# Layer 0 of a two-layer trunk: other places for the scan turns, the first gate blocks and the first out-projection blocks

## The chip, the cores and the metric

The kernel runs on one core of one Trainium2 chip. The metric is the device time of one execution in microseconds (us); several executions give a median.

## The reference, cut to what matters

A trunk of two layers works on x of 1024 positions by 1024 channels in float32. Layer 0 is a state-space mixer (SSD), layer 1 a retention mixer; each is added to the residual stream, and a final norm follows. The change touches layer 0 and the start of its out-projection:

```
z, xbc, dt = split(rmsnorm(x) @ w_in)        # 2048 + 4096 + 32 columns
xs, B, C   = split(silu(causal_conv4(xbc)))  # 2048 + 1024 + 1024
y = ssd_scan(xs, softplus(dt + bias), B, C)  # chunks of 128, 8 groups of 4 heads
y = (y + d_skip * xs) * silu(z)
y = group_rmsnorm(y, 8 groups)
h = x + y @ w_out                            # contraction over 2048
```

Within a chunk the scan needs products of C and B weighted by a decay, and across chunks a state that is carried from one chunk to the next.

## The kernel before, in words

**Data and blocks.** Channels lie on partitions, positions on the free axis. Every product in float32 is made of three matmuls (mm3, L143): operand high by high, high by low, low by high, where high and low are an FP32R copy on ScalarE (L109) and the rest on VectorE (L110). A *block part* is one 128-column slice of w_in: B, C, two x slices and two z slices per group. Each block part is made in two *half blocks*, one for each half of the positions: 24 matmuls of 128x512 into one PSUM bank of the tag mm, which has three banks (project, L239). VectorE scales each bank by the norm's factor as it leaves PSUM (L342 for B, C and x; L363 for the gate z).

**Convolution.** After its second half block a B, C or x part goes through the causal convolution (conv_unit, L330): ScalarE starts an accumulator of the tag acc (L345), VectorE adds three taps (L347), ScalarE takes a tanh (L349), and VectorE finishes silu (L350). The tag acc has two buffers, and the norm's two squares use the same tag (L513).

**Turns of the scan.** Each of the 8 groups has 4 turns (visit, L441) of two chunks. A turn makes the state products pst (L461), then the PE part of the *next* turn's front (front_pe, L388: transposes of X and B and the product of B and C, L396 to L398), then the outputs py (L485, L491). The next turn's front on the other engines follows (front, L401): scaled copies of X (L414, L416), ScalarE's decay products (L425 to L433) and VectorE's products (L434, L436). The decays are loaded from DRAM by load_decay (L380, queue of SP) into the tag acb with two buffers, two turns at a time. The last turn of a group needs B, C and x of the following group, since it makes that group's first front.

**Norm of a group.** norm (L507) has three steps: the product with the gate (L511); squares on ScalarE and their sum on GpSimd (L515, L516); then matmuls pn with a matrix of ones (L522), a logarithm and an exponential on ScalarE (L523, L524), the scaling (L527) and the store to DRAM (L530, to ysp).

**The order.** Layer0.run (L533) merges generators: merge (L71) always advances the one with the smallest (steps done + 0.5) / length. In stage g (0 to 6) it merges the six block parts of the list steps[g + 1] (B, C, x, x of group g + 1 and z, z of group g; 12 half blocks, 10 in stage 0), the 4 turns of group g and the norm of group g - 1. In manual_schedule (L558) TensorE issues in this written order. All other engines and queues, and TensorE outside that part, are ordered by a planner that simulates the program; a buffer of a tag is waited for when all are in use.

**Start.** B and C of group 0 come first; then decay() (L259: the softplus of dt on VectorE and ScalarE, the running sums pcum and ptot on TensorE, both in mm banks, L303 to L306) is merged with x(0,0), x(0,1) and z(0,0) (L554). Then the front of the first turn is made (L559).

**Tail.** The last stage has the two z parts of group 7, its four turns, the norms of groups 6 and 7, and the first steps of the out-projection (OutProj, L575). One step of the out-projection is half of the contraction (8 of 16 slices) of one 128-row block of h for one half of the positions: 24 matmuls. A block's two halves follow one another in the same mm bank, and take_h (L675) adds the residual as the bank is read. The y values come back from ysp by DMA (load, L585: two slices each, y0 to y7) and are split into high and low. Loads y0 and y1 are issued ahead (start, L978), y2 to y6 as the contraction reaches them, and y7, which holds group 7, last (L610).

The merges of the stages, before:

```
lst = self.steps[g + 1]
gens = [(self.units(lst), 2 * len(lst)), (take(vs, 4), 4)]
if g:
    gens.insert(0, (self.norm(g - 1, 0, T), 4))
merge(*gens)
```

Of the kernel before, what the change touches and what calls it, by code (L numbers as in the profile page):

```python
# [20 lines left out]
P = 128  # L21
T = 1024
D = 1024
KT = D // P
NC = T // P
HALF = 512
# [42 lines left out]


def merge(*seqs):  # L71
    gens = [[iter(g), n, 0] for g, n in seqs]
    while gens:
        gens.sort(key=lambda e: (e[2] + 0.5) / e[1])
        e = gens[0]
        try:
            next(e[0])
            e[2] += 1
        except StopIteration:
            gens.pop(0)  # L80


def take(gen, n):
    for _ in range(n):
        if next(gen, StopIteration) is StopIteration:
            return
        yield


def urgent(tc, gen):  # L90
    while True:
        with tc.high_priority():
            if next(gen, StopIteration) is StopIteration:
                return
        yield
# [7 lines left out]
def drain(gen):  # L103
    for _ in gen:
        pass
# [7 lines left out]
class WStream:  # L113


    def __init__(self, nc, cx, srcs, ahead, name, pools=None):
        self.nc, self.cx, self.srcs, self.ahead, self.name = nc, cx, srcs, ahead, name
        self.pools = pools or [(cx.gp, 2)]
        self.ring = [pl for pl, n in self.pools for _ in range(n)]
        self.ready, self.next = [], 0  # L120
# [22 lines left out]
def mm3(nc, ps, ahi, alo, bhi, blo, first, last):  # L143
    nc.tensor.matmul(ps, ahi, bhi, start=first, stop=False)  # L144
    nc.tensor.matmul(ps, ahi, blo, start=False, stop=False)  # L145
    nc.tensor.matmul(ps, alo, bhi, start=False, stop=last)  # L146


class Layer0:
    def __init__(self, tc, cx):  # L150
        self.tc, self.cx, nc = tc, cx, tc.nc
        self.nc = nc
        con = cx.con
        self.es = ExitStack()
        self.ps = self.es.enter_context(tc.tile_pool(name="ps0", bufs=1, space=PSUM))
        self.sb = self.es.enter_context(tc.tile_pool(name="sb0", bufs=1, side="right"))
        self.ident = con[:, CO["ident"] : CO["ident"] + P]
        self.ones, self.ones_r = cx.ones, cx.ones_r
        self.tri = con[:, CO["tri"] : CO["tri"] + P]
        idx = {}  # L160
        for g in range(SSD_G):
            for j in range(2):
                idx[("z", g, j)] = 2 * g + j
                idx[("x", g, j)] = 16 + 2 * g + j
            idx[("B", g)] = 32 + g
            idx[("C", g)] = 40 + g
        self.steps = [[("B", 0), ("C", 0), ("x", 0, 0), ("x", 0, 1), ("z", 0, 0)]]
        for g in range(SSD_G):
            nxt = [("B", g + 1), ("C", g + 1), ("x", g + 1, 0), ("x", g + 1, 1)] if g + 1 < SSD_G else []
            self.steps.append(nxt + ([("z", g, 0), ("z", g, 1)] if g else [("z", 0, 1)]))  # L170
        seq = [s for st in self.steps for s in st]
        self.ws = WStream(nc, cx, [cx.w0[idx[s]] for s in seq], 1, "w0")
        self.S = [dict() for _ in range(SSD_G)]
        self.rstd = self.tile([P, T], "rstd", 1, "rstd0")
        self.dt_ps, self.first_banks = {}, []
# [357 lines left out]
    def run(self, tail, start):  # L533

        nc, cx = self.nc, self.cx
        self.load_x()
        self.split_x(0)
        self.dt_project(0)
        self.squares(0)
        first, second = self.units([("B", 0)]), self.units([("C", 0)])  # L540
        fb = self.ps.tile([P, 2, 512], F32, tag="pa", bufs=1, name="fb")
        self.first_banks = [fb[:, 0, :], fb[:, 1, :]]
        next(first)
        next(second)
        self.stats(0)
        self.split_x(1)
        self.dt_project(1)
        self.squares(1)
        next(first)
        next(second)  # L550
        self.stats(1)
        drain(first)
        drain(second)
        merge((self.decay(), 3), (self.units(self.steps[0][2:]), 2 * len(self.steps[0][2:])))  # L554
        for q in range(2):
            self.load_decay(0, q)
        vs = self.visits()
        with self.tc.manual_schedule(engines={mybir.EngineType.PE}):  # L558
            self.fr = self.front(0, 0, self.front_pe(0, 0))  # L559
            for g in range(SSD_G - 1):  # L560
                lst = self.steps[g + 1]
                gens = [(self.units(lst), 2 * len(lst)), (take(vs, 4), 4)]
                if g:
                    gens.insert(0, (self.norm(g - 1, 0, T), 4))
                merge(*gens)
            g = SSD_G - 1
            start()
            merge((self.norm(g - 1, 0, T), 4), (self.units(self.steps[g + 1]), 4), (take(vs, 2), 2))
        merge((take(vs, 1), 1), (self.norm(g, 0, HALF), 3), (take(tail, 1), 1))
        merge((vs, 1), (take(tail, 3), 3))  # L570
        merge((self.norm(g, HALF, T), 3), (tail, 4))
        self.es.close()


class OutProj:  # L575
    def __init__(self, tc, cx, wsrc, ysrc, name, slots, early, raw, evac):
        self.raw = raw
        self.tc, self.cx, self.nc = tc, cx, tc.nc
        self.ws = WStream(
            tc.nc, cx, [wsrc[d][i] for _ in range(2) for d in range(KT) for i in range(2)], 1, name  # L580
        )
        self.ysrc, self.name, self.slots, self.early, self.evac = ysrc, name, slots, early, evac
        self.ys = {}

# [13 lines left out]

    def gen(self):
        nc, cx = self.nc, self.cx  # L600
        for h in range(2):
            for d in range(KT):
                pt = cx.mm_tile(f"{self.name}p{h}_{d}")
                for i in range(2):
                    w = self.ws.get()
                    for kk in range(8):
                        k = 8 * i + kk
                        if kk % 2 == 0:
                            for a in range(k // 2, min(k // 2 + 2, 8)):
                                if h or a < 7 or k == 14:  # L610
                                    self.load(h, a)
                        hi, lo = self.ys[h, k // 2]
                        ks = slice(kk * P, (kk + 1) * P)
                        mm3(nc, pt, w[0][:, ks], w[1][:, ks], hi[:, k % 2, :], lo[:, k % 2, :], k == 0, k == 15)
                    if i == 1:
                        self.evac(h, d, pt)
                        a = d - (KT - 1 - len(self.early))
                        if h == 0 and 0 <= a < len(self.early):
                            self.load(1, a, self.early[a])
                    yield  # L620


class Rope:
# [43 lines left out]
class Layer1:  # L667
# [46 lines left out]
    def start(self):  # L714
        tc, cx = self.tc, self.cx
        self.es = ExitStack()
        self.ps = self.es.enter_context(tc.tile_pool(name="psL", bufs=1, space=PSUM))
        self.sb = self.es.enter_context(tc.tile_pool(name="sbL", bufs=1, reuse_waits="tile"))
        self.es.enter_context(tc.tile_pool(name="spad", bufs=1)).tile([P, 48], F32, name="spad")
        self.gB = self.es.enter_context(tc.tile_pool(name="gB", bufs=1, reuse_waits="tile"))  # L720
        seq = []
        for h in range(RH):
            seq += [cx.w1qk[4 * h + i] for i in range(4)]
            seq += [cx.w1g[4 * h + i] for i in range(4)]
            seq += [cx.w1v[4 * h + i] for i in range(4)]
        self.ws = WStream(self.nc, cx, seq, 1, "w1", [(cx.gp, 2), (self.gB, 3)])
# [211 lines left out]
def body(tc, aps):  # L938
    nc = tc.nc
    cx = Ctx()  # L940
# [3 lines left out]
    with ExitStack() as es:  # L944
# [27 lines left out]
        cx.act = act_es.enter_context(tc.tile_pool(name="actp", bufs=1))  # L972
        l0 = Layer0(tc, cx)
        l1 = Layer1(tc, cx)
        op0 = OutProj(tc, cx, aps["w0o"], cx.ysp, "o0", lambda i: (cx.act, "act", 16), [], lambda h: (l0.sb, "yT", 4), l1.take_h)
        g0 = op0.gen()

        def start():  # L978
# [108 lines left out]
```

## Time and profile before

| | us |
|---|---|
| Median of 3 runs | 1778.81 |
| Lowest and highest run | 1775.88, 1779.36 |
| The profiled execution's own time | 1781.39 |
| Its span in the trace | 1779.6 |
| TensorE busy in it | 1715.4 |
| VectorE busy | 1086.1 |
| ScalarE busy | 697.1 |

The span is what the trace covers, from the first to the last instruction; the execution's own time has a little around it. Engines are called PE (TensorE matmul), PEld (its weight load), DVE (VectorE), ACT (ScalarE), POOL (GpSimd) and SP (SyncE, which issues most DMAs). PEclk is the clock granted to TensorE as a share of 2.4 GHz. L12 is line 12 of the kernel. A wait is put down to what ended it last.

### The profile page before, as it was taken

Reading aid. Unit: us, or ns where it says so; the run is one execution under the profiler, and the core shown is the slowest. Engines: PE = TensorE matmul, PEld = TensorE weight load, DVE = VectorE, ACT = ScalarE, POOL = GpSimd, SP = SyncE. Lnnn points to the kernel's source line nnn. Section 1 sums busy time; section 2 is a strip of 40 time slices with the busy share of each in tenths; the row PEclk is TensorE's granted clock in tenths of the full one; section 3 lists DMA queues with packets and bytes.
Section 4 is the critical chain, followed back from the end, with each engine's and each line's share of the span. In section 5 each row is a group of like instructions: output and inputs, shape, how many; then the busy total and the mean of one; then the engine's idle time right before and its main releaser. Section 6 shows DMA issues by size and latency. Waiting matters only on the chain.

```text
span 1779.6 us, 21284 instructions
## 1 busy us (share of the span) xinstructions
PE 1715.4 (96%) x8382; PEld 1403.9 (79%) x8382; DVE 1086.1 (61%) x1681; ACT 697.1 (39%) x1066; POOL 100.8 (6%) x109
## 2 busy tenths in 40 slices
PE   8799999999999999899999999999999999999996
PEld 5677878787878787788878888888888888888885
DVE  7767677777777778667644157436624661666443
ACT  6344455454545455645431223132213322333422
POOL 3010101010101011100000000000000000000000
PEclk9899999999999999999999999999999999999998
DMA  5151222222222223456441102111211211344452
GB/s 181 34 104 63 60 83 61 83 71 72 72 80 63 83 61 95 143 185 217 142 151 51 48 13 77 54 48 33 75 36 54 66 51 45 112 134 140 152 177 78
DMA packets 74357, 157.69 MB, mean 89 GB/s; under 512 B 7568, under 2 KB 24592, under 8 KB 74256
## 3 DMA queue, kind: packets, MB, share of 16 engines
q1 hardware_dynamic: 72960, 154.09, 27.4%
q10 hardware_dynamic: 1296, 2.23, 0.3%
q8 instruction: 66, 1.08, 0.3%
q14 instruction: 35, 0.29, 0.1%
HBM read 130.99 MB, written 25.30 MB: 88 GB/s over the span
## 4 chain that ended last, share of the span: by engine, by line
PE 78%; DVE 11%; ACT 6%; DMA 3%; issue 1%; SPq 0%; DVEq 0%; ACTq 0%
PE ip L144 6%; PE ip L145 6%; PE ip L146 6%; PE o1p L146 3%; PE g L146 3%; PE g L145 3%; PE o1p L144 3%; PE g L144 3%; PE o1p L145 3%; PE v L144 3%; PE v L145 3%; PE v L146 3%; PE o0p L145 3%; PE o0p L146 3%; PE o0p L144 3%; DVE acc L347 2%
## 5 line engine op out<-in xcount | busy, mean ns | idle before, releaser
L144 PE MATMUL ip<-hh,w0h 128*128 128x512 f32 x496 | 196.8, 397 | 1.4 <-DVE pre L342 1.4
L145 PE MATMUL ip<-hl,w0h 128*128 128x512 f32 x496 | 194.6, 392 | 0.0
L146 PE MATMUL ip<-hh,w0l 128*128 128x512 f32 x496 | 193.9, 391 | 0.0
L110 DVE TENSOR_TENSOR w1l<-w1r,w1h 128x1024 fp32r<-128x1024 f32 x48 | 58.3, 1222 | 147.5 <-ACT w1h L109 146.9
L347 DVE SCALAR_TENSOR_TENSOR acc<-pre,vec,acc 128x1024 f32<-128x1024 f32 x96 | 122.5, 1278 | 6.6 <-ACT acc L345 5.9
L109 ACT CAST w0h<-w0r 128x1024 fp32r<-128x1024 f32 x48 | 50.4, 1049 | 188.4 <-PE ip L145 157.9
L144 PEld LDWEIGHTS ip<-hh,w0h 128*128 128x128 f32 x496 | 93.7, 189 | 24.6 <-issue 1.9
L145 PEld LDWEIGHTS ip<-hl,w0h 128*128 128x128 f32 x496 | 93.8, 189 | 20.2 <-DVE hl L215 0.8
L146 PEld LDWEIGHTS ip<-hh,w0l 128*128 128x128 f32 x496 | 93.7, 189 | 20.0 <-issue 0.2
L144 PE MATMUL o0p<-o0yh,o0h 128*128 128x512 f32 x256 | 101.5, 397 | 3.4 <-ACT o0yh L109 2.2
L342 DVE TENSOR_TENSOR pre<-ip,rstd 128x512 f32<-128x512 f32 x62 | 42.6, 688 | 101.2 <-PE ip L146 101.1
L109 ACT CAST w1h<-w1r 128x1024 fp32r<-128x1024 f32 x48 | 50.1, 1051 | 137.5 <-PE q L145 53.1
L146 PE MATMUL o0p<-o0yh,o0l 128*128 128x512 f32 x256 | 101.9, 398 | 0.6 <-DVE o0l L110 0.6
L144 PE MATMUL z<-hh,w0h 128*128 128x512 f32 x256 | 102.5, 400 | 0.0
L145 PE MATMUL o0p<-o0yl,o0h 128*128 128x512 f32 x256 | 101.1, 395 | 0.8 <-DVE o0yl L110 0.8
L144 PE MATMUL v<-w1h,h 128*128 128x512 f32 x256 | 101.6, 398 | 0.0
L146 PE MATMUL o1p<-o1yh,o1l 128*128 128x512 f32 x256 | 100.1, 392 | 0.4 <-DVE o1l L110 0.4
L145 PE MATMUL v<-w1l,h 128*128 128x512 f32 x256 | 100.3, 392 | 0.0
L146 PE MATMUL v<-w1h,h 128*128 128x512 f32 x256 | 100.1, 391 | 0.0
L144 PE MATMUL g<-w1h,h 128*128 128x512 f32 x256 | 100.0, 391 | 0.0
L146 PE MATMUL z<-hh,w0l 128*128 128x512 f32 x256 | 99.8, 390 | 0.0
L144 PE MATMUL o1p<-o1yh,o1h 128*128 128x512 f32 x256 | 99.6, 390 | 0.2 <-DVE vl L791 0.2
(242 smaller groups left out, 4000.3 us busy)
## 6 DMA issues: line engine op xcount, KB each, us to landing
w0r<-w SPq DMA_DIRECT2D x48, 512.0 KB, 3.3
acb<-acd SPq DMA_DIRECT2D x16, 1024.0 KB, 8.0
o0r<-w0o SPq DMA_DIRECT2D x32, 512.0 KB, 3.3
o1r<-w1o SPq DMA_DIRECT2D x32, 512.0 KB, 3.2
o0yr<-ysp SPq DMA_DIRECT2D x32, 256.0 KB, 3.4
w1r<-w1qk SPq DMA_DIRECT2D x16, 512.0 KB, 3.3
w1r<-w1g SPq DMA_DIRECT2D x16, 512.0 KB, 3.3
w1r<-w1v SPq DMA_DIRECT2D x16, 512.0 KB, 3.2
```

The costliest lines, as they stand in the source:

```text
L109: nc.scalar.copy(hi, src)
L110: nc.vector.tensor_tensor(lo, src, hi.bitcast(F32), ALU.subtract)
L144: nc.tensor.matmul(ps, ahi, bhi, start=first, stop=False)
L145: nc.tensor.matmul(ps, ahi, blo, start=False, stop=False)
L146: nc.tensor.matmul(ps, alo, bhi, start=False, stop=last)
L342: nc.vector.tensor_tensor(pre[:, 3 + h * HALF : 3 + (h + 1) * HALF], pt, self.rstd[:, sl], ALU.mult)
L347: nc.vector.scalar_tensor_tensor(acc, pre[:, j : j + T], cw(j), acc, ALU.mult, ALU.add)
```

## The change

1. merge takes a third value for a generator in place of 0.5. Turns and norms of the stages now have 1.0: their steps come when a full quarter of the stage's half blocks is issued, the last at the stage's end. In the last stage the turns have 1.0, then 0.7.
2. z(0,0) leaves the merge with decay() and goes into stage 0, behind x of group 1. The front of the first turn is made after both half blocks of B(1), which are drawn ahead of the stage's merge.
3. The out-projection of layer 0 takes the first half of the contraction of its blocks 0, 1 and 2 first (three banks open at once), then the second half of each, then the other blocks as before. The out-projection of layer 1 keeps its order.
4. The merges of the last two turns move into the part where TensorE issues in the written order.

```
 def merge(*seqs):
-    gens = [[iter(g), n, 0] for g, n in seqs]
+    gens = [[iter(q[0]), q[1], 0, q[2] if len(q) > 2 else 0.5] for q in seqs]
     while gens:
-        gens.sort(key=lambda e: (e[2] + 0.5) / e[1])
+        gens.sort(key=lambda e: (e[2] + e[3]) / e[1])
...
-        self.steps = [[("B", 0), ("C", 0), ("x", 0, 0), ("x", 0, 1), ("z", 0, 0)]]
+        self.steps = [[("B", 0), ("C", 0), ("x", 0, 0), ("x", 0, 1)]]
...
-            self.steps.append(nxt + ([("z", g, 0), ("z", g, 1)] if g else [("z", 0, 1)]))
+            self.steps.append(nxt + [("z", g, 0), ("z", g, 1)])
...
         with self.tc.manual_schedule(engines={mybir.EngineType.PE}):
-            self.fr = self.front(0, 0, self.front_pe(0, 0))
             for g in range(SSD_G - 1):
-                lst = self.steps[g + 1]
-                gens = [(self.units(lst), 2 * len(lst)), (take(vs, 4), 4)]
+                u = self.units(self.steps[g + 1])
+                n = 2 * len(self.steps[g + 1])
+                if g == 0:
+                    drain(take(u, 2))
+                    self.fr = self.front(0, 0, self.front_pe(0, 0))
+                    n -= 2
+                gens = [(u, n), (take(vs, 4), 4, 1.0)]
                 if g:
-                    gens.insert(0, (self.norm(g - 1, 0, T), 4))
+                    gens.insert(0, (self.norm(g - 1, 0, T), 4, 1.0))
                 merge(*gens)
             g = SSD_G - 1
             start()
-            merge((self.norm(g - 1, 0, T), 4), (self.units(self.steps[g + 1]), 4), (take(vs, 2), 2))
-        merge((take(vs, 1), 1), (self.norm(g, 0, HALF), 3), (take(tail, 1), 1))
-        merge((vs, 1), (take(tail, 3), 3))
+            merge((self.norm(g - 1, 0, T), 4), (self.units(self.steps[g + 1]), 4), (take(vs, 2), 2, 1.0))
+            merge((self.norm(g, 0, HALF), 3), (take(tail, 1), 1), (take(vs, 1), 1, 0.7))
+            merge((take(tail, 1), 1), (vs, 1))
         merge((self.norm(g, HALF, T), 3), (tail, 4))
...
-        self.ws = WStream(
-            tc.nc, cx, [wsrc[d][i] for _ in range(2) for d in range(KT) for i in range(2)], 1, name
-        )
+        self.seq = [(0, d, i) for i in range(2) for d in range(lead)]
+        self.seq += [(0, d, i) for d in range(lead, KT) for i in range(2)]
+        self.seq += [(1, d, i) for d in range(KT) for i in range(2)]
+        self.ws = WStream(tc.nc, cx, [wsrc[d][i] for _, d, i in self.seq], 1, name)
...
-        for h in range(2):
-            for d in range(KT):
-                pt = cx.mm_tile(f"{self.name}p{h}_{d}")
-                for i in range(2):
-                    w = self.ws.get()
+        pts = {}
+        for h, d, i in self.seq:
+            if i == 0:
+                pts[d] = cx.mm_tile(f"{self.name}p{h}_{d}")
+            pt = pts[d]
+            w = self.ws.get()
...
```

The default of lead is 1, which is the order before; layer 0's out-projection is made with lead 3. The body of gen is otherwise the same.

## Rows read from the trace of the kernel before

**Rows 1.** The page: its head line and TensorE's busy time.
```profile
span 1779.6 us, 21284 instructions
...
PE 1715.4 (96%) x8382; PEld 1403.9 (79%) x8382; DVE 1086.1 (61%) x1681; ACT 697.1 (39%) x1066; POOL 100.8 (6%) x109
```

**Rows 2.** Waits of PE, 100 to 701 us: total, times, longest.
```profile
PE pa L396 <- DVE pre L350: 20.7, 7, 4.0
PE py L485 <- DVE acb L434: 3.9, 1, 3.9
```

**Rows 3.** Windows: length, busy PE, PEld, DVE, ACT, POOL, then PEclk, DMA, GB/s.
```profile
182.20:617.75 435.55, 421.27 (x2331) 348.89 (x2331) 317.84 (x385) 213.05 (x346) 50.71 (x55) 0.98 0.24 73
182.20:267.80 85.60, 82.75 (x467) 68.42 (x467) 63.56 (x77) 42.61 (x70) 9.95 (x11) 1.00 0.26 74
160.00:182.00 22.00, 21.10 (x113) 17.88 (x114) 11.25 (x15) 6.01 (x15) 0.20 (x2) 0.92 0.23 72
721.60:765.00 43.40, 38.84 (x205) 30.23 (x202) 29.50 (x41) 26.07 (x42) 6.65 (x5) 0.92 0.44 147
```

**Rows 4.** Timeline of PE: start, length, line, operation, idle time before it and releaser.
```profile
69.61 0.47 PE L396 MATMUL pa<-con,pre 128*128 128x128 f32 x1 [9.31 <-DVE pre L350]
...
102.86 1.38 PE L485 MATMUL py<-acb,xdt 128*64 128x128 f32 x12 [3.91 <-DVE acb L434]
...
106.48 0.41 PE L146 MATMUL ip<-hh,w0l 128*128 128x512 f32 x1
...
222.41 1.88 PE L522 MATMUL pn<-nsq,ones_r 128*128 128x512 f32 x4
224.13 1.03 PE L461 MATMUL pst<-xde,bn 128*128 128x256 f32 x4
...
228.08 0.50 PE L144 MATMUL z<-hh,w0h 128*128 128x512 f32 x1
...
244.56 0.59 PE L461 MATMUL pst<-xde,bn 128*128 128x256 f32 x2
...
248.11 0.33 PE L396 MATMUL pa<-con,pre 128*128 128x128 f32 x1 [2.85 <-DVE pre L350]
...
684.82 0.48 PE L396 MATMUL pa<-con,pre 128*128 128x128 f32 x1 [3.99 <-DVE pre L350]
...
690.40 0.50 PE L144 MATMUL z<-hh,w0h 128*128 128x512 f32 x1
...
710.53 1.88 PE L522 MATMUL pn<-nsq,ones_r 128*128 128x512 f32 x4
```

**Rows 5.** Timeline of DVE, single rows between 182 and 731 us.
```profile
182.21 0.69 DVE L342 TENSOR_TENSOR pre<-ip,rstd 128x512 f32<-128x512 f32 x1 [4.75 <-PE ip L146]
...
194.86 1.23 DVE L350 SCALAR_TENSOR_TENSOR pre<-pre,acc 128x1024 f32<-128x1024 f32 x1 [0.53 <-ACT pre L349]
...
239.45 1.21 DVE L350 SCALAR_TENSOR_TENSOR pre<-pre,acc 128x1024 f32<-128x1024 f32 x1
...
259.66 1.23 DVE L511 TENSOR_TENSOR yT<-yT,w 128x1024 f32<-128x1024 f32 x1
...
730.24 1.23 DVE L110 TENSOR_TENSOR o0yl<-o0yr,o0yh 128x1024 fp32r<-128x1024 f32 x1
```

**Rows 6.** Timeline of ACT, single rows between 223 and 285 us.
```profile
223.45 1.28 ACT L523 ACT_TABLE_LOAD   x1
224.75 0.69 ACT L523 ACTIVATE nsq<-pn,cst 128x512 f32<-128x512 f32 x1
...
267.59 1.05 ACT L109 CAST w0h<-w0r 128x1024 fp32r<-128x1024 f32 x1 [9.29 <-PE ip L145]
...
283.11 1.24 ACT L345 ACTIVATE acc<-pre,vec 128x1024 f32<-128x1024 f32 x1
284.25 1.05 ACT L515 ACTIVATE nsq<-yT 128x1024 f32<-128x1024 f32 x1
```

**Rows 7.** Timeline of POOL, the sum of the norm's squares in one stage.
```profile
209.02 2.40 POOL L516 TENSOR_TENSOR nsq<-nsq,nsq 128x1024 f32<-128x1024 f32 x1 [0.15 <-ACT nsq L515]
```

More of the change, by code (lines that the diff above doesn't have):

```diff
@@ L575, with __init__ @@
 class OutProj:
-    def __init__(self, tc, cx, wsrc, ysrc, name, slots, early, raw, evac):
+    def __init__(self, tc, cx, wsrc, ysrc, name, slots, early, raw, evac, lead=1):
         self.raw = raw
         self.tc, self.cx, self.nc = tc, cx, tc.nc
-        self.ws = WStream(
-            tc.nc, cx, [wsrc[d][i] for _ in range(2) for d in range(KT) for i in range(2)], 1, name
-        )
+        self.seq = [(0, d, i) for i in range(2) for d in range(lead)]
+        self.seq += [(0, d, i) for d in range(lead, KT) for i in range(2)]
+        self.seq += [(1, d, i) for d in range(KT) for i in range(2)]
+        self.ws = WStream(tc.nc, cx, [wsrc[d][i] for _, d, i in self.seq], 1, name)
         self.ysrc, self.name, self.slots, self.early, self.evac = ysrc, name, slots, early, evac
@@ L600, in gen @@
         nc, cx = self.nc, self.cx
-        for h in range(2):
-            for d in range(KT):
-                pt = cx.mm_tile(f"{self.name}p{h}_{d}")
-                for i in range(2):
-                    w = self.ws.get()
[L606 to L620, printed above, removed]
+        pts = {}
[4 more added lines that the diff above has]
+            w = self.ws.get()
+            for kk in range(8):
+                k = 8 * i + kk
+                if kk % 2 == 0:
+                    for a in range(k // 2, min(k // 2 + 2, 8)):
+                        if h or a < 7 or k == 14:
+                            self.load(h, a)
+                hi, lo = self.ys[h, k // 2]
+                ks = slice(kk * P, (kk + 1) * P)
+                mm3(nc, pt, w[0][:, ks], w[1][:, ks], hi[:, k % 2, :], lo[:, k % 2, :], k == 0, k == 15)
+            if i == 1:
+                self.evac(h, d, pt)
+                a = d - (KT - 1 - len(self.early))
+                if h == 0 and 0 <= a < len(self.early):
+                    self.load(1, a, self.early[a])
+            yield
 class Rope:
@@ L974, in body @@
         l1 = Layer1(tc, cx)
-        op0 = OutProj(tc, cx, aps["w0o"], cx.ysp, "o0", lambda i: (cx.act, "act", 16), [], lambda h: (l0.sb, "yT", 4), l1.take_h)
+        op0 = OutProj(tc, cx, aps["w0o"], cx.ysp, "o0", lambda i: (cx.act, "act", 16), [], lambda h: (l0.sb, "yT", 4), l1.take_h, 3)
         g0 = op0.gen()
```

## The prediction

> **What bounds the kernel now.** I read the page first [rows 1]: TensorE is busy for 1715.4 of 1779.6 us, so the change can only win TensorE's idle time, 64 us, and the time its matmuls run at half clock. That profiled execution took 1781.39 us; the median of the three runs is 1778.81, 2.6 us lower, and I set the sum against the median.
>
> Second, the table of TensorE's waits between 100 and 701 us, the group loop of layer 0 [rows 2]. It holds two lines: the transposes of front_pe waited for the last convolution step of x (L350) seven times, 20.7 us in all, and py waited once, 3.9 us.
>
> Third, the stages [rows 3]. The stage from 182.2 to 267.8 us ran at full clock: 85.60 us, of them 82.75 busy. The five stages from 182.2 to 617.75 us have 421.27 us of busy TensorE with the same work; 5 x 82.75 is 413.75, so 7.5 us are matmuls stretched by a lower clock after the wait.
>
> Fourth, TensorE in order of time [rows 4]. At 248.11 stands such a wait (2.85 us) inside the last turn of a group: the next group's X is not ready. At 684.82 the longest (3.99): what follows runs at half rate (1.2 of 2.4 GHz; its first transpose takes 0.48 us, that of 248.11 takes 0.33) until 690.40. From here too come the unit prices: 222.41 to 224.13, the norm's matmuls pn, 1.72 us; 224.13 to 228.08, one scan turn, 3.95; 228.08 to 244.56, three half blocks, 5.49 each.
>
> **The order by hand.** I worked merge() through on paper, with u0 to u11 for a stage's half blocks (B, C, x0, x1, z0, z1, two each), v for turns, n for norm steps. Before: u0 u1 n1 v0, u2 u3 u4 v1 n2, u5 u6 u7 n3 v2, u8 u9 u10 v3, u11. After: u0 u1 u2 n1 v0, u3 u4 u5 v1 n2, u6 u7 u8 n3 v2, u9 u10 u11 v3. All turns stay three half blocks apart; against x1's end (u7), v3 now comes after four half blocks, not three.
>
> **Why X is late.** The tag acc has two buffers, shared by the convolutions and the norm's squares. It hands them out in program order: the square's input was ready at 259.66 + 1.22 and ScalarE idled 9.29 us before 267.59, yet the square ran at 284.25, right behind C's acc of 283.11 [rows 5, 6]. So before, both squares precede x0, and x0 and x1 wait for pn. x0's convolution, the first behind pn, ends at 239.45 + 1.2 = 240.6, which is 18.2 us after pn begins [rows 4, 5]; x1's comes still later and stalls the turn.
>
> After, x0 takes its buffer ahead of the squares, and x1 has x0's old place. From pn to the last turn TensorE then has 1.72 + 3.95 + 16.48 = 22.2 us of work against 18.2: 4.0 us to spare, so all seven waits go. The gain is 20.7 idle, 7.5 stretched in the five stages, 22 x 0.08 = 1.8 for the first boundary [rows 3] and (690.40 - 684.82) / 2 = 2.8 for the last: **-32.8 us**. Bounds: the waits stay (0), or all go; no more is there.
>
> In that chain ScalarE switches its function table twice, and the rows price a switch at 1.28 us, the next activation starting 0.02 us after it [rows 6]. The Trainium skill, page "ScalarE: Activation LUTs", section on what ACT_TABLE_LOAD costs, puts a switch at about 2.66 us with its drain. By that the slack would be some 2.8 us smaller, an estimate from that page: the sum would stay, and rival 2 below would be some 5 points likelier. The row decides, and I leave the chance as it is.
>
> **The new order's own wait.** The squares now follow x0. The nearest case is B's convolution beside turn v0: its last product lands at 182.21 and L350 ends at 194.86 + 1.23, 13.9 us on [rows 5]. Then a square (1.05) [rows 6] and the sum on POOL (2.40) [rows 7]: 17.4 us. pn is reached after 3.95 + 16.48 = 20.4 us. Cover 3.0 us, or 1.9 if a weight cast (1.05) goes first. **0 us**; if the cover is gone, each microsecond costs six, since stages 1 to 6 repeat it.
>
> **First turn.** py waited 3.91 us for the decay products, then ran at half rate to 106.48 [rows 4]: 3.91 + 3.62 / 2 = 5.7. After, three half blocks stand between front(0,0) and v0 instead of one, 11.0 us more against 3.9. **-5.7 us** (bounds 0 and -5.7).
>
> **Start.** TensorE idles 9.31 us before 69.61 [rows 4], with x's last half block runnable, since pcum and ptot come first in the bank tag mm. With z(0,0) gone from that merge, pcum stands ahead of both halves of x(0,1), so one more half block falls behind the idle time: **+5.5 us**. Bounds: +5.5, or -5.5 if the planner lets both halves run inside the wait; I take the first, as the same row shows the tag's order holding. B(1) takes z(0,0)'s place, so no work is added.
>
> **Tail.** Between 721.6 and 765 us TensorE idles 43.40 - 38.84 = 4.6 us and loses up to 0.08 x 43.4 = 3.5 to the clock [rows 3], waiting for y loads. After, t1, turn 30, pn, t2, turn 31 stand in TensorE's written order, and y7 is first wanted two half contractions later, so that wait goes. But t1 comes one z block earlier, right behind turn 29. It needs y3, split 730.24 + 1.23 - 710.53 = 20.9 us after group 6's pn [rows 4, 5], while TensorE reaches t1's end 1.72 + 5.49 + 3.95 + 5.49 = 16.7 us after pn: some 5 us idle plus clock. One goes, one comes: **0 us**, bounds -8.1 and +6.
>
> **Queues.** z(0,0)'s weight load moves behind B(1)'s on SP; same count. The decay loads on SP keep three half blocks (16 us and a turn) before use. The loads y5 to y7 are issued two blocks later on SP, inside the tail's bounds. POOL's products for the state move with the turns; the norm's sum on POOL is priced above. What TensorE idles elsewhere is untouched.
>
> Sum: -32.8 - 5.7 + 5.5 + 0 = -33.0; 1778.8 - 33.0 = **1746 us**.
>
> **Rivals.**
> 1. **pn waits for x0 and the squares** (20 in 100). For: cover of only 1.9 to 3.0 us, and VectorE's order is the planner's. Against: B's case fits. A wait of 2 us in six stages, with the 1.5 us of stretched matmuls (7.5 / 5) each: +21, so 1767; down to 1752 with 1 us and no clock loss.
> 2. **X stays late** (11 in 100): the planner lets the squares go ahead of x0 after all, x1 stays last and six boundaries remain. Then only the first boundary (under 20.7 / 7 + 1.8 = 4.8) and py are won: -4.8 - 5.7 + 5.5 = -5, so 1774. Against: ScalarE's idle stretch with the square held back.
> 3. **Slower** (6 in 100): the same place as rival 1, but x0's convolution takes over 20.4 + 4.0 - 3.5 = 20.9 us instead of 13.9, because turn v1's products and the residue of the weights are served first on VectorE. From a 4.0 us wait on, 6 x (4.0 + 1.5) eats the gain of 33; at 7 us it is 51, so 1797.
> 4. **Nothing moves** (5 in 100): the wait reappears, equally long, at the first matmuls of v0, or the tail gives everything back: 1779.
>
> **Numbers.** Forecast 58 in 100, its own range 1737 to 1752. A measurement of this kernel can tell about 0.2%, 3.6 us, from no change. Rival 2 lies near that line; I give 6 of its 11 to faster. Faster 58 + 20 + 6 = 84, same 5 + 5 = 10, slower 6. The range takes the forecast with both bounds of tail and start (1778.8 - 32.8 - 5.7 - 8.1 = 1732, with the start at nothing) and rival 1 up to 1767: 78 in 100.
>
> **What would show it.** Right: no wait of pa for L350 past 100 us, spans of 83 us per stage at clock 1.00, the first idle stretch near 15 us. Wrong: pn listed as waiting for POOL (rival 1 or 3), pa still waiting (rival 2), a start under 9 us idle, or a tail idle well off 5 us.

## The result, and the profile after

The changed kernel takes **1746.94 us** (median of 4 runs, 1744.77 to 1748.22), against 1777.93 for the kernel before: a ratio of 0.9825, 95% interval 0.9808 to 0.9842, so 31.0 us less. The forecast was 1746, the range 1732 to 1767. The profiled execution of after is its lowest run (1744.77), and that of before (1781.39) [rows 1] lies above its other runs, so the two traces differ by more than the medians: 36.9 us of span.

The page of after, head line and TensorE's busy time:

```profile
span 1742.7 us, 21293 instructions
PE 1698.3 (97%) x8382; PEld 1390.7 (80%) x8382; DVE 1085.7 (62%) x1681; ACT 698.5 (40%) x1066; POOL 93.8 (5%) x109
```

Against [rows 1], the same 8382 matmuls cost 1715.4 - 1698.3 = 17.1 us less, at a mean granted clock of 0.991 in place of 0.983, and TensorE idles 44.4 us instead of 64.2: 19.8 less. Most of both comes from waits that are gone and from the lower clock behind them. Lines in after stand 1 further down (L351 is L350 of before), in the out-projection and layer 1 up to 7.

The waits of PE in after (total, times, longest), first 0 to 100 us, then from 680 us. Between 100 and 680 us the same view lists nothing, where [rows 2] had eight waits:

```profile
PE pcum L305 <- DVE t_a L299: 14.6, 1, 14.6
...
PE py L486 <- DVE acb L435: 3.5, 1, 3.5
PE o0p L146 <- DVE o0yl L111: 1.6, 2, 0.8
PE o0p L147 <- DVE o0l L111: 1.4, 1, 1.4
```

The seven waits of pa and the first turn's wait of py are gone. What is left is one longer wait at the start (9.3 before) and a few at the last turns and behind them.

Windows of after (columns as in [rows 3]): one stage, the five stages that answer to 182.2 to 617.75 of before, then the tail in two pieces:

```profile
182.61:265.13 82.52, 82.52 (x468) 68.50 (x467) 63.10 (x78) 42.79 (x69) 9.10 (x11) 1.00 0.24 77
182.61:595.64 413.03, 413.03 (x2334) 342.88 (x2333) 315.97 (x386) 214.01 (x345) 45.50 (x55) 1.00 0.24 77
...
690.00:735.00 45.00, 39.87 (x241) 32.27 (x240) 31.36 (x41) 26.77 (x44) 7.69 (x6) 0.96 0.42 146
735.00:765.00 30.00, 29.96 (x130) 24.11 (x129) 23.29 (x34) 14.68 (x17) 0.00 (x0) 1.00 0.63 212
```

The five stages have no idle time and the full clock: 413.03 us against 435.55 in [rows 3], 22.5 less.

TensorE of after in order of time (start, length, line, operation, idle before and releaser): the start, one stage, and the last turns:

```profile
70.12 1.20 PE L305 MATMUL pcum<-t_a,con 128*128 128x256 f32 x2 [14.62 <-DVE t_a L299]
...
202.60 1.02 PE L462 MATMUL pst<-xde,bn 128*128 128x256 f32 x4
...
223.01 1.88 PE L523 MATMUL pn<-nsq,ones_r 128*128 128x512 f32 x4
224.72 1.03 PE L462 MATMUL pst<-xde,bn 128*128 128x256 f32 x4
...
245.15 0.59 PE L462 MATMUL pst<-xde,bn 128*128 128x256 f32 x2
245.58 0.38 PE L397 MATMUL pa<-con,pre 128*128 128x128 f32 x2
...
700.49 1.02 PE L462 MATMUL pst<-xde,bn 128*128 128x256 f32 x4
...
706.14 0.69 PE L486 MATMUL py<-acb,xdt 128*64 128x128 f32 x4 [3.53 <-DVE acb L435]
```

From pn (223.01) to the stage's last turn (245.15) TensorE has 22.1 us of work, and pa follows at 245.58 without a wait. The three other engines in that stage, DVE, ACT and POOL:

```profile
202.80 0.69 DVE L343 TENSOR_TENSOR pre<-ip,rstd 128x512 f32<-128x512 f32 x1 [2.53 <-PE ip L147]
...
214.90 1.22 DVE L351 SCALAR_TENSOR_TENSOR pre<-pre,acc 128x1024 f32<-128x1024 f32 x1
...
240.16 1.22 DVE L351 SCALAR_TENSOR_TENSOR pre<-pre,acc 128x1024 f32<-128x1024 f32 x1
```

```profile
216.15 1.06 ACT L516 ACTIVATE nsq<-yT 128x1024 f32<-128x1024 f32 x1 [1.81 <-DVE pre L351]
...
224.58 1.28 ACT L524 ACT_TABLE_LOAD   x1
225.88 0.69 ACT L524 ACTIVATE nsq<-pn,cst 128x512 f32<-128x512 f32 x1
```

```profile
217.29 2.40 POOL L517 TENSOR_TENSOR nsq<-nsq,nsq 128x1024 f32<-128x1024 f32 x1 [9.41 <-ACT nsq L516]
```

x0's convolution ends at 216.12 and its end releases the second square at 216.15: the squares now stand behind x0. The sum is ready at 219.69, 3.3 us ahead of pn. x1's convolution ends at 241.38, 4.2 us ahead of pa.

### The profile page after: what moved, and what is told of

Read it like the earlier page. It is cut to its first block, busy times and chain, and to the rows that moved or that the text cites. A ratio compares the mean times of both kernels' runs of the same rounds, so it can differ in the third digit from the quotient of the medians.

```text
span 1742.7 us, 21293 instructions
## 1 busy us (share of the span) xinstructions
PE 1698.3 (97%) x8382; PEld 1390.7 (80%) x8382; DVE 1085.7 (62%) x1681; ACT 698.5 (40%) x1066; POOL 93.8 (5%) x109
## 4 chain that ended last, share of the span: by engine, by line
PE 89%; DVE 4%; ACT 3%; DMA 2%; issue 1%; SPq 0%; DVEq 0%; ACTq 0%
PE ip L145 7%; PE ip L146 6%; PE ip L147 6%; PE o1p L147 3%; PE g L145 3%; PE g L147 3%; PE o1p L145 3%; PE g L146 3%; PE o1p L146 3%; PE z L145 3%; PE z L147 3%; PE z L146 3%; PE v L145 3%; PE v L146 3%; PE v L147 3%; PE o0p L147 3%
## 5 line engine op out<-in xcount | busy, mean ns | idle before, releaser
L145 PE MATMUL g<-w1h,h 128*128 128x512 f32 x256 | 100.1, 391 | 0.0
L147 PE MATMUL g<-w1h,h 128*128 128x512 f32 x256 | 99.8, 390 | 0.0
```

## Experiments

Each edit is made to the changed kernel unless it says otherwise. Runs 1 to 4, 5 to 8 and 9 to 12 each shared their runs of the kernel before (medians 1778.76, 1778.61 and 1778.24).

| run | median, us | ratio to before, interval |
|---|---|---|
| 1 turns and norms at the half (10 runs) | 1777.39 | 0.9988 (0.9974 to 1.0001) |
| 2 norms alone at the end | 1753.99 | 0.9864 (0.9848 to 0.9881) |
| 3 turns alone at the end | 1751.83 | 0.9850 (0.9835 to 0.9865) |
| 4 before, with a third acc buffer | 1752.65 | 0.9855 (0.9840 to 0.9870) |
| 5 lead 1 | 1748.58 | 0.9837 (0.9815 to 0.9859) |
| 6 both halves of x(0,1) ahead of the sums | 1734.21 | 0.9762 (0.9740 to 0.9784) |
| 7 z(0,0) back at the start | 1740.69 | 0.9793 (0.9774 to 0.9812) |
| 8 as 6, with priority for the last turns | 1734.93 | 0.9760 (0.9737 to 0.9784) |
| 9 tail of before | 1743.96 | 0.9809 (0.9795 to 0.9824) |
| 10 as 6, with the tail of before | 1734.22 | 0.9758 (0.9742 to 0.9775) |
| 11 as 6, last two merges left to the planner | 1735.95 | 0.9764 (0.9748 to 0.9780) |
| 12 as 11, last stage's turns at the half | 1732.93 | 0.9747 (0.9733 to 0.9762) |

**Runs 1 to 3: which shift carries the gain?**

```
-                gens = [(u, n), (take(vs, 4), 4, 1.0)]
+                gens = [(u, n), (take(vs, 4), 4)]             # runs 1 and 2
...
-                    gens.insert(0, (self.norm(g - 1, 0, T), 4, 1.0))
+                    gens.insert(0, (self.norm(g - 1, 0, T), 4))   # runs 1 and 3
```

> The changed kernel with the turns and norms of stages 0 to 6 back at one half (norm 0.5, turns 0.5); the start, the last stage and the out-projection stay changed. Theory (the seven boundary waits are the whole gain, start, first turn and tail cancel): about 20 us of waits of the transposes for the last convolution step come back, with a lower clock behind some of them, and the time is 1747 + 33 = 1780 us, no faster than before. Rival (a good part of the gain comes from the last stage and the out-projection): it stays below 1770 us.

Measured: 1777.39, the gain is gone. Its ten runs spread from 1769.78 to 1779.78, the lowest at a mean granted clock of 0.988, the highest at 0.982. Its waits of PE, 100 to 701 us:

```profile
PE pa L397 <- DVE pre L351: 18.3, 6, 4.0
...
```

Six boundary waits are back. The seventh, the first boundary's (2.45 us at 160.90 in before), is not: it goes by the new stage 0 and not by the shift. So the places of turns and norms are nearly all that the change wins in sum; the start, the first turn, the first boundary and the tail cancel to within a few microseconds.

> The changed kernel with the norms late (1.0) but the turns at one half (0.5). x0 has its accumulator ahead of the squares, as in the changed kernel, but the last turn comes only two half blocks after pn. Theory (X is ready some 18 us after pn begins, and the last turn must come later than that): from pn to the last turn there are 1.7 + 11.0 = 12.7 us of work, so the transposes wait about 5.5 us in each of six stages, some 36 us with the first boundary, plus the clock behind them: 1795 us or more, slower than before. Rival (the order of the two accumulator buffers alone is what matters): the waits are gone, 1747 us.

Measured: 1753.99. The theory missed by over 40 us; the rival is nearer, 7 us off, but small waits stay. Waits, 100 to 701 us, then one boundary on PE and the end of x1's convolution on DVE:

```profile
PE pa L397 <- DVE pre L351: 5.9, 6, 1.3
...
227.68 1.88 PE L523 MATMUL pn<-nsq,ones_r 128*128 128x512 f32 x4
240.32 0.59 PE L462 MATMUL pst<-xde,bn 128*128 128x256 f32 x2
241.95 0.33 PE L397 MATMUL pa<-con,pre 128*128 128x128 f32 x1 [0.93 <-DVE pre L351]
```

```profile
240.68 1.22 DVE L351 SCALAR_TENSOR_TENSOR pre<-pre,acc 128x1024 f32<-128x1024 f32 x1
```

The last turn stands 12.6 us after pn, as worked out on paper, but X is ready 241.90 - 227.68 = 14.2 us after pn, not 18.2. Here turn v2 stands ahead of pn, and the front that it makes on VectorE (L415 to L437) lies ahead of that stretch (221.69 to 226.38); in after it lies within it (229.34 to 238.52). The 18.2 us held a turn, and were no constant of the convolution. Putting x0's buffer ahead of the squares thus wins 1777.39 - 1753.99 = 23.4 us with the turns left where they were.

> The changed kernel with the turns late (1.0) but the norms at one half (0.5). The squares take both accumulators ahead of x0 as in the kernel before, so x1 is ready some 25.6 us after pn begins; from pn to the last turn there are 1.7 + 5.5 + 4.0 + 16.5 = 27.7 us of work. Theory: 2 us to spare, no waits, 1747 us as the changed kernel: the later turn is enough. Rival (the squares must follow x0, or x1 stays late): waits of 2 to 5 us per stage remain, 1760 to 1775 us.

Measured: 1751.83, the expected 1747 and 5 us more. No pa waits, but a new wait instead (100 to 701 us, then DVE around one of them, whose turn begins at 224.31 on PE):

```profile
PE py L492 <- DVE S L475: 7.4, 6, 1.2
```

```profile
224.25 2.48 DVE L528 SCALAR_TENSOR_TENSOR yT<-yT,vec,nsq 128x1024 f32<-128x1024 f32 x2 [0.34 <-ACT nsq L525]
226.65 1.28 DVE L348 SCALAR_TENSOR_TENSOR acc<-pre,vec,acc 128x1024 f32<-128x1024 f32 x1
227.84 0.68 DVE L364 TENSOR_TENSOR w<-z,rstd 128x512 f32<-128x512 f32 x1
228.44 0.41 DVE L475 TENSOR_TENSOR S<-S,pst 128x256 f32<-128x256 f32 x1
```

With the norm alone left early, its scaling (L528) comes up on VectorE just as the turn begins, and the state's sum is queued behind it and two more instructions. So either shift alone wins most of the gain, and the other one its last 5 to 7 us.

**Run 4: are the two shared buffers the cause?** The kernel before, with a third acc buffer; padding in the memory was shortened to make room (that alone wasn't run).

```
-        acc = self.tile([P, T], "acc", 2, f"acc{ci}")
+        acc = self.tile([P, T], "acc", 3, f"acc{ci}")
...
-        sq = [self.tile([P, T], "acc", 2, f"nsq{g}_{j}_{lo}") for j in range(2)]
+        sq = [self.tile([P, T], "acc", 3, f"nsq{g}_{j}_{lo}") for j in range(2)]
```

> The kernel before, with three buffers of the tag acc in place of two (the padding tiles cut to 64 bytes to make room), order untouched. x0 then takes a buffer without waiting for pn, and x1 takes the first square's right after pn, in the place that x0 had. Theory (the two shared buffers hold X back): X is ready 18.2 us after pn against 22.2 us of work, so the waits of stages 1 to 6 go (18 us and the clock behind them, some 28 us); the first boundary (2.5 us), the start (9.3 us) and the first turn (3.9 us) stay: about 1750 us. Rival (VectorE's queue, not the buffers, makes X late): the waits stay near 2.9 us each, 1778 us.

Measured: 1752.65, 2.7 above the expected 1750. Waits, 100 to 701 us:

```profile
PE py L485 <- DVE acb L434: 4.3, 1, 4.3
PE pa L396 <- DVE pre L350: 2.5, 1, 2.5
PE py L491 <- DVE S L474: 1.8, 6, 0.3
```

The start of x0's convolution on ScalarE in the stage from 182 us on, first in run 4, then in before:

```profile
212.82 1.24 ACT L345 ACTIVATE acc<-pre,vec 128x1024 f32<-128x1024 f32 x1
```

```profile
225.33 1.23 ACT L345 ACTIVATE acc<-pre,vec 128x1024 f32<-128x1024 f32 x1
```

With the order of before, one buffer more takes 20.7 us of pa waits down to 2.5. x0's convolution starts 10 us ahead of pn in run 4 (pn at 222.77), and 3 us behind it in before (222.41). X was late because it waited for a buffer; the shortened padding would hardly move that start to the other side of pn.

**Runs 6 and 7: the start.** Run 6 takes both halves of x(0,1) ahead of pcum and ptot; run 7 undoes part 2 of the change in the lists of steps.

```
-        merge((self.decay(), 3), (self.units(self.steps[0][2:]), 2 * len(self.steps[0][2:])))
+        us, dec = self.units(self.steps[0][2:]), self.decay()
+        drain(take(us, 1))
+        drain(take(dec, 1))
+        drain(us)
+        drain(dec)
```

> The changed kernel with both half blocks of x(0,1) written ahead of the running sums pcum and ptot at the start. Theory (the banks of the tag mm go out in written order, so a sum that is written earlier holds back half blocks that could run): the idle stretch of 14.6 us before pcum shrinks by two half blocks, 11 us, to about 4 us: 1736 us. Rival (the softplus chain on VectorE is pushed back by the convolution that now starts earlier): the sums come 3 to 5 us later, 1740 us. Second rival (the planner had chosen the order itself): 1747 us.

> The changed kernel with z(0,0) back in the first merge, so that the sums stand behind the first half block of x(0,1) again. Theory (the start's price is one half block of idle time): the idle stretch falls from 14.6 to about 9.3 us, 1741.5 us. Rival (the start has no price, since what idles less there waits later, at the first turn): 1747 us.

Measured: 1734.21 and 1740.69, both within 2 us of what was expected. The waits of PE for pcum, first of run 6, then of run 7:

```profile
PE pcum L305 <- DVE t_a L299: 4.9, 1, 4.9
```

```profile
PE pcum L305 <- DVE t_a L299: 9.8, 1, 9.8
```

Each half block that stands behind pcum costs 4.8 to 4.9 us of idle time (14.6, 9.8, 4.9), and 6.3 to 6.5 us by the medians. The spans of the three traces (1742.7, 1738.9, 1732.4) give 3.8 and 6.5, so what a half block costs beyond its idle time stays open.

**Runs 5 and 8 to 12: the tail.** Run 5 sets lead to 1. Run 8 gives the last turns priority in the planner. Runs 9 and 10 have the last stage of before:

```
-            merge((self.norm(g - 1, 0, T), 4), (self.units(self.steps[g + 1]), 4), (take(vs, 2), 2, 1.0))
-            merge((self.norm(g, 0, HALF), 3), (take(tail, 1), 1), (take(vs, 1), 1, 0.7))
-            merge((take(tail, 1), 1), (vs, 1))
+            merge((self.norm(g - 1, 0, T), 4), (self.units(self.steps[g + 1]), 4), (take(vs, 2), 2))
+        merge((take(vs, 1), 1), (self.norm(g, 0, HALF), 3), (take(tail, 1), 1))
+        merge((vs, 1), (take(tail, 3), 3))
...
-... l1.take_h, 3)
+... l1.take_h, 1)
```

Run 11 only moves the last two merges out of the written part; run 12 also drops the 1.0 of the first of the three.

> The changed kernel with the out-projection's blocks in the order of before (a block's two half contractions one after the other), all else changed. The second out-projection step then stands in the written order ahead of the last turn and needs the last y, which is ready some 16 us after the last pn; ahead of that need there are about 4 us of work. Theory (the three first halves are what covers the way of the last y through DRAM): 10 to 14 us of waiting come back, 1757 to 1763 us. Rival (the tail is hidden anyway): 1747 us.

Measured: 1748.58, against 1746.94 with lead 3, intervals that overlap. The theory's 10 us and more did not come. Turns are counted from 0 over all groups, so 30 and 31 are the last two. In this run's timeline of PE three half contractions stand between them, where the written order has one: the planner placed free ones there. Turn 31 begins at 726.22, not 716.97:

```profile
705.44 0.70 PE L486 MATMUL py<-acb,xdt 128*64 128x128 f32 x4 [3.53 <-DVE acb L435]
...
726.22 0.59 PE L462 MATMUL pst<-xde,bn 128*128 128x256 f32 x2
```

> As the run with the sums last, and the planner is also told to put the last stage's turns first, so that ScalarE makes the decay products of turn 30 ahead of the copies of y. Theory (turn 30's products queue behind those copies: 3.5 us of waiting): that wait goes, and at most 1 to 2 us of it come back as a later y: 1733 to 1735 us. Rival (the copies of y then are late by as much): no change against the run with the sums last.

Measured: 1734.93. The planner put every engine's instructions in the order of run 6, so this is a repeat of run 6 (0.7 us off) and no test of the wait.

> The changed kernel with the last stage as the kernel before has it: the last two turns and the last norm at the half, the two last merges outside the written part, and the out-projection's free half contractions with a lead of 1; all other stages as changed. Theory (the tail is worth nothing either way): within 3 us of the changed kernel, 1744 to 1750 us, with the waits of 680 to 860 us about those of the kernel before. Rival (the new tail pays): 1751 us or more. Second rival (the new tail costs): 1742 us or less.

> The kernel that puts both half blocks of the first norm ahead of the running sums (1734.2 us), with the last stage of the kernel before. Theory (the tail is worth nothing either way): 1731 to 1737 us. Rivals as in the run with the tail back alone: 1738 or more if the new tail pays, 1730 or less if it costs.

Measured: 1743.96 and 1734.22. Run 9 is 3.0 us below the changed kernel, with overlapping intervals, and falls a hair below the theory's 1744 without reaching the second rival's 1742; run 10 equals run 6. Nowhere does the new tail pay; at most it costs 3 us. Waits of run 9, 680 to 860 us:

```profile
PE o0p L145 <- ACT o0h L110: 1.4, 1, 1.4
PE py L492 <- DVE S L475: 0.9, 1, 0.9
PE o0p L147 <- DVE o0l L111: 0.8, 1, 0.8
PE o0p L146 <- DVE o0yl L111: 0.8, 1, 0.8
...
```

With a last one of 0.5 that is 4.4 us of small waits, against 6.5 in after.

> The kernel that puts both half blocks of the first norm ahead of the running sums (1734.2 us), with the last two merges taken out of the written part, so that free out-projection work may be placed in them by the planner, lead 3 kept. The waits for turn 30's product (3.5 us) and for the out-projection's inputs (1.6 us) can fall away. Theory: 1729 to 1732 us. Rival (what is drawn into the gap is missing behind it, and another wait takes its place): 1733 to 1736 us.

> As the run before it (last two merges outside the written part, lead 3), and the last stage's two turns at the half instead of at the ends. Theory (the turn's products get more time ahead of the blocks that use them, and free work fills what is left): 1729 to 1732 us. Rival (nothing of this tail is worth anything measurable): 1733 to 1736 us.

Measured: 1735.95 and 1732.93. In run 11 turn 30's product is still waited for, 3.5 us: the planner drew nothing into that gap, and why stays open. In run 12 that wait falls to 0.3 us, but py now waits 2.4 us for the state's sum (L475): on VectorE that sum starts at 692.07, right behind the split of a y load (690.93), which itself had waited 0.94 us for ScalarE's copy of it. Run 11 lands in its rival's range, though not by the rival's mechanism, since the same wait is still there; run 12 is 1.3 us below run 6, less than the intervals can tell apart.

## Why the prediction was right

**Boundaries (-32.8).** Right. All seven waits are gone, the five stages take 413.03 us where 413.75 was worked out, and run 1 shows that the six boundaries behind the first are nearly the whole net gain (1777.39 - 1746.94 = 30.5 of 31.0 us). The chain behind it came out as priced in this order: X ready 18.4 us after pn (18.2 forecast), 22.1 us of work up to the turn (22.2), 3.3 us of cover for pn (3.0), and 216.12 - 202.80 = 13.3 us from x0's last product to the end of its convolution (13.9). None of the rivals came about: pn waits for nothing, x0 takes its buffer ahead of the squares, its convolution is no slower than B's was, and no wait appears at the first matmuls of v0.

**Why X was late.** Right, and shown from two sides: run 4 (a buffer more) and run 2 (x0 ahead of the squares). What I had not seen is that the buffer order alone wins most: I carried the 18.2 us as if it belonged to X, and forecast run 2 with it, 40 us too slow. It is 14.2 us where no turn follows pn. The prediction was spared by luck: its order has the same turn in that place as the one the figure was read from.

**The function tables.** In after a switch is 1.28 us with the next activation 0.02 us behind it (224.58 to 225.88), as in [rows 6], and the chain came out at 18.4 us with two of them. The Trainium skill, page "ScalarE: Activation LUTs", section on what ACT_TABLE_LOAD costs, gives 2.66 us for load and drain; the measurement decides, and no drain shows here. Taking a further 2.8 us off the slack would have been wrong in any case: the 18.2 us were read from a chain that already held two switches (223.45 and 227.16 in before), just as they ran.

**First turn (-5.7).** Right: no wait of py is left there.

**Start (+5.5).** Right: TensorE idles 14.62 us for 9.31, and runs 7 and 6 confirm the mechanism, in that each half block ahead of pcum takes 4.8 to 4.9 us off the idle time. It is also where the change left most on the table.

**Tail (0).** Right in size, wrong in the main cause. The forecast was some 5 us idle for y3 against the wait for y7 gone. Between 690 and 735 us after idles 45.00 - 39.87 = 5.1 us, and from there to 765 nothing (one wait of 1.4 us for a split weight follows at 770.91). But only 1.6 us of it wait for split y values. The largest, 3.53 us, is turn 30's product acb, a step I had not priced: one half contraction stands between that turn and the one before, where the stages have three half blocks. VectorE of after at that point:

```profile
701.40 1.21 DVE L437 TENSOR_TENSOR ce<-ce,pre 128x1024 f32<-128x1024 f32 x1
702.54 0.68 DVE L512 TENSOR_TENSOR yT<-yT,w 128x512 f32<-128x512 f32 x1
703.14 1.21 DVE L111 TENSOR_TENSOR o0yl<-o0yr,o0yh 128x1024 fp32r<-128x1024 f32 x1
704.27 0.68 DVE L512 TENSOR_TENSOR yT<-yT,w 128x512 f32<-128x512 f32 x1
704.88 1.21 DVE L435 TENSOR_TENSOR acb<-acb,cbm 128x1024 f32<-128x1024 f32 x1
```

ScalarE's part of acb (L434) is done at 702.59; the norm's products and a y split go first on VectorE, 704.88 - 702.54 = 2.3 us of them. Runs 5, 9 and 10 show that neither lead 3 nor the written order of the last turns earns anything measurable.

**The sum.** The stretched matmuls of my terms are 7.5 + 1.8 + 2.8 + 1.8 = 13.9 us; TensorE's busy time fell by 17.1. The 3.2 us between stand in none of my terms. By groups of matmuls, the out-projection of layer 0 takes 3.1 us less than in before, layer 1's q 1.8 less, and dt at the start 2.0 more; why layer 1 gains, which the change leaves alone, no run shows.

**The best version.** Run 6 (1734.21) beats both kernels, 12.7 us below the changed one; with run 12's tail 1732.93 was measured.

## What to carry to other kernels

Where a tile tag has few buffers, read when each user takes its buffer in program order, not only when it has its data: a consumer that is early in time but takes its buffer late can hold the whole pipeline. Here one step moved, or one more buffer, cured it. A latency read between two events holds all that the queues served in between, so it can be carried only to an order that has the same work between them. Behind the first long wait of a kernel, look for work that is ready and stands behind the waiting instruction only through the order of a bank.

## What the runs showed of the hardware

**GpSimd and VectorE hold each other up.** The state's product on GpSimd, same tile and shape, takes 1.53 us or 0.61 in one stage of after:

```profile
204.23 1.53 POOL L474 TENSOR_TENSOR S<-S,cdb 128x256 f32<-128x256 f32 x1 [14.70 <-DVE S L475]
...
226.36 0.61 POOL L474 TENSOR_TENSOR S<-S,cdb 128x256 f32<-128x256 f32 x1 [6.66 <-DVE S L475]
...
229.56 0.61 POOL L474 TENSOR_TENSOR S<-S,cdb 128x256 f32<-128x256 f32 x1 [2.55 <-DVE S L475]
```

```profile
204.07 1.22 DVE L111 TENSOR_TENSOR w0l<-w0r,w0h 128x1024 fp32r<-128x1024 f32 x1
...
218.63 2.14 DVE L111 TENSOR_TENSOR w0l<-w0r,w0h 128x1024 fp32r<-128x1024 f32 x1 [0.17 <-ACT w0h L110]
...
229.67 0.68 DVE L417 TENSOR_TENSOR xdt<-pa,dth 128x512 f32<-128x512 f32 x1
```

The slow product runs beside a VectorE weight split (204.07 to 205.29), the one of 226.36 within a pause of VectorE (226.28 to 227.80). The other way round, the same weight split takes 2.14 us beside GpSimd's sum of squares (217.29 to 219.69) and 1.22 us at 204.07, although GpSimd works there too. In both pairs the one that began second is the slow one, by 0.92 us where the first still had 1.06 us to run. The product of 229.56 is not slowed, though VectorE is busy beside it: the split reads two tiles in SBUF, but xdt has one of its two inputs (pa) in PSUM. The Trainium skill, page "GPSIMD Engine Reference", section 1 on specifications, says that the two engines share their SBUF interfaces, with contention where a VectorE instruction has two SBUF inputs; the rows agree. No run took one engine's part away, so the cause itself is not shown.

**The clock after short waits.** In the last stage of after two waits of 0.77 and 0.83 us left the output matmuls behind them at the full rate; after the one of 3.53 us they ran at half (0.64 us for a row of four instead of 0.39, a granted clock of 0.50 from 706.20 to 709.20) for some 3 us. The length of a wait doesn't settle it. Five waits of before are alike, 2.85 to 2.86 us: behind that of 248.11 in [rows 4] the granted clock stayed at 1.00 up to 254.00, behind that of 595.14 it was 0.50 up to 601.00, behind that of 420.94 the half rate came at once and lasted some 3 us, and behind those of 333.72 and 507.93 it came only after 1.2 to 1.4 us. So one and the same wait costs a different time from stage to stage.
